# First norms of a fp32 encoder trunk: loads reordered, zero products on TensorE, operands written straight from PSUM, and sums of x placed later

## The chip, the cores and the metric

The kernel runs on one core of a Trainium2 chip. The metric is the device time of one execution in microseconds. A core has five engines that run their own instruction queues and wait for each other by semaphores: TensorE (PE in the profile, with its weight loads as PEld), VectorE (DVE), ScalarE (ACT), GpSimd (POOL) and SyncE (SP, which here only issues DMAs). ACT and POOL issue some DMAs too.

## The reference

Two sequences, 512 and 256 tokens of 1024 channels, go through the same two layers:

```python
def run_trunk(x, norm_g, final_norm_g, ffn_w1, ffn_w2, ...):
    for li in range(DEPTH):                      # DEPTH = 2
        x = x + 0.5 * swiglu_ffn(rmsnorm(x, norm_g[li, 0]), ffn_w1[li, 0], ffn_w2[li, 0])
        h = rmsnorm(x, norm_g[li, 1])
        x = x + (hgrn2_mixer(h, ...) if li == 0 else window_gqa_mixer(h, ...))
        x = x + 0.5 * swiglu_ffn(rmsnorm(x, norm_g[li, 2]), ffn_w1[li, 1], ffn_w2[li, 1])
    return rmsnorm(x, final_norm_g)

def rmsnorm(x, g):      # in float32
    return x * lax.rsqrt(jnp.mean(x * x, axis=-1, keepdims=True) + 1e-6) * g

def swiglu_ffn(x, w1, w2):
    gate, up = jnp.split(x @ w1, 2, axis=-1)     # w1: 1024 x 5632
    return (jax.nn.silu(gate) * up) @ w2         # w2: 2816 x 1024
```

So there are four feed-forward blocks (called f0 to f3 below), two token mixers and seven norms. The change touches the first norm, the start of f0, and one step of all four feed-forward blocks.

## The kernel before, in words

All 768 tokens are handled together as six blocks of 128 (`x[0]` to `x[5]`, 128 x 1024 each, in SBUF for the whole kernel); blocks 0 to 2 are half 0 and 3 to 5 half 1. A float32 product is made of three TensorE products: each operand is split into a high part (`hi`, rounded to the matmul's type) and a low part (`lo`, the difference), and `mm3` (L262 to L264) multiplies hi by hi, hi by lo, lo by hi. ACT makes the high part (L267, a cast), DVE the low part (L268, a subtraction); for weights the same is done at L170 and L171, and L203 and L204.

The kernel starts like this. `setup` loads an identity matrix (SP, L101) and casts it on DVE (L103); it loads the norm gains and some other vectors as rows into one tile (`cols`, three DMAs on ACT's queue, L109), turns them by a TensorE transpose (L112) and copies them out of PSUM on DVE (L114). `load_x` loads x (L278) and the first weights (L155). `norm_block` normalizes a block: ACT squares it and sums the row (L304), ACT takes the root (L305), DVE inverts it (L306) and scales x (L307) into `xn`. `turn` transposes four of the eight 128-channel columns of a half's three blocks (PE, L324), and multiplies by the gain while it copies out of PSUM (ACT, L327) into a plain tile `tn`. The six operands come from `tn`: first the parts of half 0 by `put`, which splits a pair of columns of 128 x 768 (L267, L268). In PE's order the plain products `up_plain` of half 0 come first, and between them, on fixed columns, `run_later` lets the deferred steps run: norms of half 1, its transposes, and `sums`.

The feed-forward products use a seven-product scheme on 2 x 2 blocks (`product`, L422), so that after the plain products sums of operands are needed: `mix` (L351 to L355, DVE on 128 x 768) and more splits; the tiles of this part are called t1 to t4. `up_pair` computes two hidden tiles with seven products, copies the first results out of PSUM on ACT (L439, L442), combines them on DVE (L448 to L461) and applies Silu (L445, L460); its tiles are split and, like the operands, mixed (L351 to L355 on 128 x 384 `tA` tiles). `down_quad` multiplies four hidden tiles back and adds to x (L508). Before its first use in a feed-forward block, six sums of quarters of x are made: three with L471 (`x12 += x22`) and three with L472 (`x21 -= x22`).

The program is written in one order, and a scheduler gives every engine its own queue from it, by when it reckons that an instruction can start; `issue_after(x)` puts instructions behind x in that order. Each engine then runs its queue strictly in order. Tiles come from rings by tag: `tB` has two buffers, so that the third tile of that tag waits until the first is free.

Of the kernel before, what the change touches and what calls it, by code (L numbers as in the profile page):

```python
# [9 lines left out]
F32 = mybir.dt.float32  # L10
F32R = mybir.dt.float32r
# [5 lines left out]
P = 128  # L17
# [25 lines left out]
RING = 1024  # L43
UP = ("p1", "p7", "p2", "p5", "p4", "p6", "p3")
# [4 lines left out]
class Trunk:  # L49
# [216 lines left out]
    def split(self, src, hi, lo):  # L266
        self.nc.scalar.copy(hi, src)  # L267
        self.nc.vector.tensor_sub(lo, src, hi.bitcast(F32))  # L268

    def load_x(self, srcs):  # L270
# [30 lines left out]
    def norm_block(self, b):  # L301
        nc = self.nc
        xn, r = self.big([P, D]), self.stat(1)
        nc.scalar.activation(xn, self.x[b], AF.Square, accum_out=r)  # L304
        last = nc.scalar.activation(r, r, AF.Sqrt, bias=self.eps, scale=1.0 / D).ins  # L305
        nc.vector.reciprocal(r, r)  # L306
        nc.vector.tensor_scalar(xn, self.x[b], r, None, ALU.mult)  # L307
        self.xn[b] = xn
        return last

    def turn(self, half, part, row):
# [8 lines left out]
        for m in range(4 * part, 4 * part + 4):  # L320
# [5 lines left out]
            if feeds_ffn:  # L326
                nc.scalar.activation(self.block(part, half, m % 4), pt, AF.Copy, scale=g)  # L327
                continue
            hi, lo = (self.h[m][:, i, half * H : (half + 1) * H] for i in range(2))
            nc.scalar.activation(hi, pt, AF.Copy, scale=g)  # L330
            nc.vector.scalar_tensor_tensor(lo, pt, g, hi.bitcast(F32), ALU.mult, ALU.subtract)  # L331
        if feeds_ffn:
            for kp in range(2):
                self.put(f"b{part}{half}", kp, self.tn[(part, half)][:, kp])
# [30 lines left out]
    xn = [None] * NBLK  # L365

# [32 lines left out]
    def up_plain(self, tag, j, half):  # L399
# [13 lines left out]
        self.nc.scalar.activation(t, pss[0], AF.Silu)  # L413
# [51 lines left out]
    def down_quad(self, tag, g, hid):  # L465
        nc = self.nc
        cols = lambda b, c: self.x[b][:, c * 512 : (c + 1) * 512]
        if g == 0:
            for i in range(HB):
                x12, x21, x22 = cols(HB + i, 0), cols(i, 1), cols(HB + i, 1)  # L470
                nc.vector.tensor_add(x12, x12, x22)  # L471
                nc.vector.tensor_sub(x21, x21, x22)  # L472
# [873 lines left out]
```

## Time and profile before

| what | value |
| --- | --- |
| time, median of 3 runs | 2764.35 us (2763.74 to 2765.22) |
| the profiled execution | 2764.33 us, of which its span is 2762.5 us and 1.83 us lie around it |
| granted TensorE clock | 0.999 of full speed over the span |
| PE busy | 2735.5 us (99%) |
| DVE, ACT, POOL busy | 2102.6 us (76%), 1326.6 us (48%), 309.4 us (11%) |
| first matmul of a product | 14.79 us after the span's start |
| first product of the seven-product scheme | 38.63 us |

The profile gives for each line of the kernel the instructions with their engine, output and inputs, how long they ran, and for how long the engine stood idle before them and for what. In the timeline a row is "start, duration, engine, line, operation", and a count `x4` merges four instructions that follow each other; the duration is then from the first one's start to the last one's end.

### The profile page before, as it was taken

To read this page: it belongs to the slowest core of one execution; us is meant where nothing else is said; L and a number is where in the kernel's file an instruction comes from. 1 tells how busy PE (TensorE), PEld (TensorE's weight loads), DVE (VectorE), ACT (ScalarE), POOL (GpSimd) and SP (SyncE) were. 2 spreads that over 40 slices of the span, in tenths; PEclk is the share of its full clock that TensorE was granted. 3 is DMA by queue.
4 is the path that set the end of the run, shared out by engine and by line. 5 is a ranking of instruction groups with operands and counts; after the bars stand their busy time and mean duration, and the time that the engine had idled before them with its cause. 6 is when DMAs were issued, how large, how long until landed. Compare 5 with 4: busy or idle time off the path is not lost.

```text
span 2762.5 us, 44483 instructions
## 1 busy us (share of the span) xinstructions
PE 2735.5 (99%) x17281; PEld 2481.5 (90%) x17281; DVE 2102.6 (76%) x3662; ACT 1326.6 (48%) x2479; POOL 309.4 (11%) x315
## 2 busy tenths in 40 slices
PE   8999999999999999999999999999999999999998
PEld 8999999888888889999999999999886789999997
DVE  7888788557477568777888878887846768788877
ACT  7444444456466354443446444444546654443444
POOL 1111211000000001121111112111000001221111
PEclk9999999999999999999999999999999999999999
DMA  5544554321110324465444355544512123555443
GB/s 160 135 117 116 138 134 119 118 67 40 55 47 25 122 62 114 112 143 133 118 120 109 83 131 138 133 115 115 146 53 77 47 62 81 134 137 128 120 112 107
DMA packets 330116, 291.63 MB, mean 106 GB/s; under 512 B 11608, under 2 KB 257840, under 8 KB 329904
## 3 DMA queue, kind: packets, MB, share of 16 engines
q1 hardware_dynamic: 294064, 212.43, 25.8%
q0 software_dynamic: 31680, 62.93, 13.4%
q10 hardware_dynamic: 4160, 13.42, 1.4%
q8 instruction: 135, 2.21, 0.3%
q14 instruction: 77, 0.63, 0.1%
HBM read 216.39 MB, written 9.44 MB: 82 GB/s over the span
## 4 chain that ended last, share of the span: by engine, by line
PE 85%; DVE 10%; ACT 3%; issue 2%; DMA 0%; DVEq 0%; ACTq 0%; SPq 0%
PE ps L422 32%; PE ps L486 21%; PE ps L262 9%; PE ps L263 9%; PE ps L264 9%; DVE w L204 2%; DVE big L268 2%; PE ps L682 1%; PE ps L1218 1%; PE ps L1157 1%; PE ps L827 1%; PE ps L1209 1%; ACT w L203 1%; DVE wr L217 1%; PE ps L324 1%
## 5 line engine op out<-in xcount | busy, mean ns | idle before, releaser
L422 PE MATMUL ps<-big,w 128*128 128x384 f32 x6720 | 1174.6, 335 | 3.4 <-ACT tA L439 2.7
L422 PEld LDWEIGHTS ps<-big,w 128*128 128x128 f32 x6720 | 1165.4, 188 | 10.9 <-ACT tA L439 9.1
L203 ACT CAST w<-wr 128x512 fp32r<-128x512 f32 x600 | 415.3, 707 | 699.8 <-DVE wr L217 376.3
L204 DVE TENSOR_TENSOR w<-wr,w 128x512 fp32r<-128x512 f32 (+1 forms) x520 | 452.8, 874 | 180.1 <-ACT w L203 153.9
L486 PE MATMUL ps<-w,big 128*128 128x512 f32 x2520 | 575.9, 389 | 1.2 <-DVE x L508 1.2
L486 PEld LDWEIGHTS ps<-w,big 128*128 128x128 f32 x2520 | 472.4, 188 | 99.6 <-ACT big L267 1.6
L508 DVE SCALAR_TENSOR_TENSOR x<-ps,x 128x512 f32<-128x512 f32 x468 | 303.5, 680 | 10.5 <-PE ps L264 10.0
L145 POOL DMA_DIRECT2D s<-wr x120 | 105.0, 875 | 1667.5 <-DMA wr<-in_ffn_w_dram 784.5
L262 PE MATMUL ps<-w,big 128*128 128x512 f32 x624 | 252.5, 405 | 0.3
L264 PE MATMUL ps<-w,big 128*128 128x512 f32 x624 | 244.6, 392 | 0.9 <-DVE big L331 0.9
L263 PE MATMUL ps<-w,big 128*128 128x512 f32 x624 | 244.4, 392 | 0.0
L262 PE MATMUL ps<-big,w 128*128 128x384 f32 (+2 forms) x640 | 219.2, 344 | 2.1 <-ACT big L267 1.3
L267 ACT CAST big<-tA 128x384 fp32r<-128x384 f32 x296 | 148.0, 513 | 149.3 <-DVE tA L454 69.0
L263 PE MATMUL ps<-big,w 128*128 128x384 f32 (+2 forms) x640 | 216.4, 338 | 0.9 <-DVE big L268 0.6
L264 PE MATMUL ps<-big,w 128*128 128x384 f32 (+2 forms) x640 | 215.6, 337 | 0.0
L268 DVE TENSOR_TENSOR big<-tA,big 128x384 fp32r<-128x384 f32 x296 | 183.0, 629 | 12.7 <-ACT big L267 11.6
L171 DVE TENSOR_TENSOR w<-wr,w 128x1024 fp32r<-128x1024 f32 x92 | 111.8, 1221 | 79.0 <-ACT w L170 73.1
L262 PEld LDWEIGHTS ps<-w,big 128*128 128x128 f32 x624 | 117.2, 188 | 29.3 <-issue 6.0
L170 ACT CAST w<-wr 128x1024 fp32r<-128x1024 f32 x92 | 96.5, 1052 | 97.8 <-PE ps L263 77.8
L204 POOL TENSOR_TENSOR w<-wr,w 128x512 fp32r<-128x512 f32 x80 | 123.3, 1541 | 177.5 <-ACT w L203 156.4
L264 PEld LDWEIGHTS ps<-w,big 128*128 128x128 f32 x624 | 117.1, 188 | 27.6 <-DVE big L331 1.7
L263 PEld LDWEIGHTS ps<-w,big 128*128 128x128 f32 x624 | 117.4, 188 | 21.8 <-issue 0.4
(163 smaller groups left out, 2899.6 us busy)
## 6 DMA issues: line engine op xcount, KB each, us to landing
wr<-in_ffn_w_dram SPq DMA_DIRECT2D x264, 512.0 KB, 3.9
s<-in_ffn_w_dram SPq DMA_DIRECT2D x120, 256.0 KB, 3.3
s<-wr POOLq DMA_DIRECT2D x120, 256.0 KB, 4.5
wr<-wr POOLq DMA_DIRECT2D x80, 256.0 KB, 3.7
wr<-in_hg_w_in_dram SPq DMA_DIRECT2D x40, 512.0 KB, 3.8
wr<-wr POOLq DMA_DIRECT2D x20, 512.0 KB, 4.6
spill<-x ACTq DMA_DIRECT2D x12, 512.0 KB, 2.7
x<-spill ACTq DMA_DIRECT2D x12, 512.0 KB, 3.3
```

The source lines that it names most:

```text
L145: self.nc.gpsimd.dma_start(out, src, accum_op=ALU.add)
L171: self.nc.vector.tensor_sub(lo, raw, hi.bitcast(F32))
L203: nc.scalar.copy(h, src)
L204: low = (eng or nc.vector).tensor_sub(l, src, h.bitcast(F32)).ins
L262: nc.tensor.matmul(out, a[0], b[0], start=first, stop=False)
L263: nc.tensor.matmul(out, a[0], b[1], start=False, stop=False)
L264: nc.tensor.matmul(out, a[1], b[0], start=False, stop=last)
L267: self.nc.scalar.copy(hi, src)
L268: self.nc.vector.tensor_sub(lo, src, hi.bitcast(F32))
L422: self.nc.tensor.matmul(ps, a[x], b[y], start=first and k == 0 and i == 0, stop=k == 3 and i == 2, skip_group_check=True,)
L486: nc.tensor.matmul(ps, a[x], w[y], start=name == chain and kp == 0 and q == 0, stop=kp == 1 and q == 2, skip_group_check=True,)
L508: self.nc.vector.scalar_tensor_tensor(x, ps, c, x, ALU.mult, ALU.add)
```

## The change

Six things are changed.

1. **Loads.** The identity is loaded by ACT's queue instead of SP's, so that SP begins with x. The small load for the attention sinks (`load_tables`) goes behind the second half's norms.
2. **Zeros.** DVE clears a 128 x 128 tile, and TensorE multiplies it by itself 15 times (L103 of the new kernel) into a PSUM bank that nobody reads. The tile is a third one of tag `tB`.
3. **A square on DVE.** Block 1's square and row sum is one DVE instruction instead of an ACT one.
4. **Straight operands.** Half 0's operands are no longer split from `tn`: ACT writes the high part and DVE the low part directly from the PSUM bank, times the gain (L345, L346), and `tn`, which `sums` still needs, is rebuilt as hi + lo by four additions on POOL (L352).
5. **Second norms.** The three norms of half 1 are ordered right behind the first half's work, and the first Silu behind them.
6. **Sums of x.** In all four feed-forward blocks the six sums before `down_quad` are put behind the last operand split (`self.mixed`).

The lines move: L101 to L114 become L105 to L120, L170/L171 become L176/L177, L203/L204 L209/L210, L262-264 L268-270, L267/L268 L273/L274, L304-L307 L313-L316, L324 L333, L327 L341, L351-355 L371-375, L413 L435, L422 L445, L439 L462, L448-L461 L471-L484, L471/L472 L495/L496, L508 L532.

```diff
@@ setup
+        zero = self.tmp(P)
+        nc.vector.memset(zero, 0.0)
         self.eps = cp.tile([P, 1], F32, name="eps")
         nc.vector.memset(self.eps, EPS)
+        idle = self.ps(P)
+        for _ in range(WARM):                                   # WARM = 15
+            nc.tensor.matmul(idle, zero, zero, start=True, stop=True)
+        raw = self.tmp(P)
+        nc.scalar.dma_start(raw, ident)
         warm = self.stat(1)
         nc.scalar.activation(warm, self.eps, AF.Sqrt)
-        raw = self.tmp(P)
-        nc.sync.dma_start(raw, ident)
@@ load_x
             with self.tc.issue_after(order) if order else nullcontext():
-                order = self.norm_block(b)
-        self.turn(0, 0, 0)
-        self.turn(0, 1, 0)
+                order = self.norm_block(b, b == 1)
+        self.turn(0, 0, 0, True)
         with self.tc.issue_after(order):
             self.stage_next()
             self.stage_next()
-        self.load_tables()
-
-        def rest():
-            for b in range(HB, NBLK):
-                self.norm_block(b)
-
-        self.later(rest, lambda: self.turn(1, 0, 0), lambda: self.turn(1, 1, 0), self.sums)
+        self.turn(0, 1, 0, True)
+        for b in range(HB, NBLK):
+            with self.tc.issue_after(order):
+                order = self.norm_block(b)
+        self.normed = order
+        with self.tc.issue_after(order):
+            self.load_tables()
+        self.later(lambda: self.turn(1, 0, 0), lambda: self.turn(1, 1, 0), self.sums)
@@ norm_block
-        nc.scalar.activation(xn, self.x[b], AF.Square, accum_out=r)
+        if on_dve:
+            nc.vector.tensor_tensor_reduce(xn, self.x[b], self.x[b], 1.0, 0.0, ALU.mult, ALU.add, r)
+        else:
+            nc.scalar.activation(xn, self.x[b], AF.Square, accum_out=r)
@@ turn
+            if straight:
+                key = (f"b{part}{half}", m % 4 // 2)
+                if key not in self.ops:
+                    self.ops[key] = self.big([P, 2, 2, H], F32R)
+                hi, lo = (self.ops[key][:, m % 2, i, :] for i in range(2))
+            elif feeds_ffn:
...
             nc.scalar.activation(hi, pt, AF.Copy, scale=g)
             nc.vector.scalar_tensor_tensor(lo, pt, g, hi.bitcast(F32), ALU.mult, ALU.subtract)
...
+            if straight:
+                self.block(part, half, 0)
+                hi, lo = (self.ops[(name, kp)][:, :, i, :].bitcast(F32) for i in range(2))
+                nc.gpsimd.tensor_add(self.tn[(part, half)][:, kp], hi, lo)
+            else:
+                self.put(name, kp, self.tn[(part, half)][:, kp])
@@ put
-        self.split(src, t[:, :, 0, :], t[:, :, 1, :])
+        self.mixed = self.split(src, t[:, :, 0, :], t[:, :, 1, :])
@@ up_plain
-        self.nc.scalar.activation(t, pss[0], AF.Silu)
+        with self.tc.issue_after(self.normed) if self.normed else nullcontext():
+            self.nc.scalar.activation(t, pss[0], AF.Silu)
+        self.normed = None
@@ down_quad
-                nc.vector.tensor_add(x12, x12, x22)
-                nc.vector.tensor_sub(x21, x21, x22)
+                with self.tc.issue_after(self.mixed):
+                    nc.vector.tensor_add(x12, x12, x22)
+                    nc.vector.tensor_sub(x21, x21, x22)
```

What the scheduler makes of it stands in the engines' queues. A row is line, operation, output and inputs, size, and in brackets the counters that it waits for; a number behind a name only tells tiles of one kind apart.

**The start, ACT.** ACT's queue from its first DMA to the first root, before:

```order
L120 DMA nsinks<-in_sw_sinks_dram 128x16
L99 ACT_TABLE_LOAD
L99 ACTIVATE stat_80<-eps 128x1 [waits DVE_49]
L109 DMA tB_86<-in_norm_g_dram 48x128
L109 DMA tB_86<-in_hg_lb_dram 32x128
L109 DMA tB_86<-in_hg_g_norm_dram 8x128
L304 ACTIVATE big_110,stat_111<-x_94 128x1024 [waits DMAHW2_49]
L305 ACTIVATE stat_111<-stat_111,eps 128x1 [waits Activation_49]
```

and now:

```order
L105 DMA tB_98<-in_ident_dram 128x128
L107 ACT_TABLE_LOAD
L107 ACTIVATE stat_100<-eps 128x1 [waits DVE_49]
L115 DMA tB_104<-in_norm_g_dram 48x128 [waits DMAHW1_49,DVE_49]
L115 DMA tB_104<-in_hg_lb_dram 32x128
L115 DMA tB_104<-in_hg_g_norm_dram 8x128
L313 ACTIVATE big_128,stat_129<-x_112 128x1024 [waits DMAHW0_49]
```

The three row loads now wait: for the identity's DMA and for DVE. `cols` is the third tile of tag `tB`, after the zeros and the raw identity.

**The start, DVE.** DVE's queue from the identity's cast to the second block's scaling, before:

```order
L103 CAST ident_r<-tB_82 128x128 [waits DMAHW1_49]
L306 RECIPROCAL stat_111<-stat_111 128x1 [waits Activation_49]
L307 TENSOR_SCALAR big_110<-x_94,stat_111 128x1024 [waits DMAHW2_49,DVE_49]
L114 COPY cols<-ps_90 128x88 [waits PE_49]
L306 RECIPROCAL stat_117<-stat_117 128x1 [waits Activation_49]
L307 TENSOR_SCALAR big_116<-x_96,stat_117 128x1024 [waits DMAHW4_49,DVE_49]
```

and now, as far as the subtraction of the second weight and past it:

```order
L109 CAST ident_r<-tB_98 128x128 [waits DMAHW1_49]
L311 ISA big_134,stat_135<-x_114 128x1024 [waits DMAHW2_49]
L120 COPY cols<-ps_108 128x88 [waits PE_49]
L315 RECIPROCAL stat_129<-stat_129 128x1 [waits Activation_49]
L316 TENSOR_SCALAR big_128<-x_112,stat_129 128x1024 [waits DMAHW0_49,DVE_49]
...
L177 TENSOR_TENSOR w_176<-wr_118,w_175 128x1024 [waits DMAHW7_49,Activation_49]
L346 SCALAR_TENSOR_TENSOR big_150<-ps_146,cols,big_150 128x384 [waits Activation_49]
...
L346 SCALAR_TENSOR_TENSOR big_163<-ps_166,cols,big_163 128x384 [waits Activation_49]
L177 TENSOR_TENSOR w_184<-wr_120,w_183 128x1024 [waits DMAHW0_49,Activation_49]
```

The copy of the gains (L114, now L120) stood behind the first block's scaling and now stands ahead of it.

**The sums of x, DVE.** The end of the stretch between operand sums and the first pair's combination, before:

```order
L448 TENSOR_TENSOR tA_593<-tA_593,ps_591 128x384 [waits PE_49]
L204 TENSOR_TENSOR w_656<-wr_400,w_656 128x512 [waits DMAHW4_49,Activation_49]
L217 TENSOR_TENSOR wr_398<-wr_398,wr_400 128x512 [waits DMASW3_49]
...
L452 TENSOR_TENSOR tA_592<-tA_592,ps_589 128x384 [waits PE_49]
...
L459 TENSOR_TENSOR tA_592<-tA_592,ps_591 128x384 [waits DVE_49,PE_49]
```

and now, with two more of the sums 16 and 20 rows above the first one shown:

```order
L471 TENSOR_TENSOR tA_615<-tA_615,ps_613 128x384 [waits PE_49]
...
L223 TENSOR_TENSOR wr_420<-wr_420,wr_422 128x512 [waits DMASW2_49]
L495 TENSOR_TENSOR x_124<-x_124 128x512
L496 TENSOR_TENSOR x_114<-x_114,x_124 128x512
L475 TENSOR_TENSOR tA_614<-tA_614,ps_611 128x384 [waits PE_49]
...
L482 TENSOR_TENSOR tA_614<-tA_614,ps_613 128x384 [waits DVE_49,PE_49]
...
L495 TENSOR_TENSOR x_126<-x_126 128x512
```

In f0, four of the six sums now stand between the operand sums and L482 (before: L459), in f1 to f3 all six. Before, all six stood ahead of the operand sums, among the norms.

More of the change, by code (lines that the diff above doesn't have):

```diff
@@ L43 @@
 RING = 1024
+WARM = 15
 UP = ("p1", "p7", "p2", "p5", "p4", "p6", "p3")
@@ L267, in split @@
         self.nc.scalar.copy(hi, src)
-        self.nc.vector.tensor_sub(lo, src, hi.bitcast(F32))
+        return self.nc.vector.tensor_sub(lo, src, hi.bitcast(F32)).ins
     def load_x(self, srcs):
@@ L309, in norm_block, with turn @@
         return last
-    def turn(self, half, part, row):
+    def turn(self, half, part, row, straight=False):
         nc = self.nc
@@ L365 @@
     xn = [None] * NBLK
+    normed = None
     def after_block(self, b, row):
```

11 lines of the change are left out of this document (5 added, 6 removed).

## The prediction

> **What bounds the kernel now.** I read the page first, then what PE waits for, then the timeline of the first 75 us.
>
> ```profile
> PE 2735.5 (99%) x17281; PEld 2481.5 (90%) x17281; DVE 2102.6 (76%) x3662; ACT 1326.6 (48%) x2479; POOL 309.4 (11%) x315
> PE ps L112 <- DMA tB<-in_hg_g_norm_dram: 7.2, 1, 7.2
> PE ps L422 <- ACT tA L439: 2.7, 11, 0.4
> ```
>
> PE is busy for 2735.5 of 2762.5 us; only 27 us can be won by waiting less. Most of what the waits show is at the start: 7.2 until the last row arrives. The one that comes back is L422 for ACT's copy L439, eleven times. So the change can move a few microseconds, in two places: the first 75 us, and the place in each feed-forward block where the second pair's first product waits for L439.
>
> The start, as the list of DMA issues (first row; 3.0 us from issue to landing) and the timeline have it:
>
> ```profile
> tB<-in_ident_dram SPq DMA_DIRECT2D x1, 64.0 KB, 3.0
> 1.25 0.38 ACTq L109 DMA_DIRECT2D tB<-in_norm_g_dram  x1
> 2.13 0.57 ACTq L109 DMA_DIRECT2D tB<-in_hg_g_norm_dram  x1
> 3.72 0.23 DVE L103 CAST ident_r<-tB 128x128 fp32r<-128x128 f32 x1 [2.85 <-DMA tB<-in_ident_dram]
> 7.23 0.38 PE L112 MATMUL ps<-ident_r,tB 88*128 88x88 f32 x1 [7.23 <-DMA tB<-in_hg_g_norm_dram]
> 7.95 0.24 DVE L114 COPY cols<-ps 128x88 f32<-128x88 f32 x1
> 8.09 5.38 PE L324 MATMUL ps<-ident_r,big 128*128 128x128 f32 x24 [0.48 <-DVE big L307]
> 10.02 0.75 DVE L307 TENSOR_SCALAR big<-x,stat 128x1024 f32<-128x1024 f32 x1
> 12.02 2.00 ACT L327 ACTIVATE big<-ps,cols 128x384 f32<-128x384 f32 x4 [0.90 <-PE ps L324]
> 15.78 0.45 PE L263 MATMUL ps<-big,w 128*128 128x384 f32 x1 [0.55 <-DVE big L268]
> 25.39 1.03 PE L324 MATMUL ps<-ident_r,big 128*128 128x128 f32 x8
> 27.72 0.75 DVE L307 TENSOR_SCALAR big<-x,stat 128x1024 f32<-128x1024 f32 x1
> 37.15 1.82 DVE L351 TENSOR_TENSOR big<-big,big 128x768 f32<-128x768 f32 x2
> ```
>
> The third norm ends at 10.77 (10.02 + 0.75), the first PSUM bank is read at 12.02, PE runs through from 15.78, the sixth norm ends at 28.47, and DVE begins the operand sums at 37.15. What comes then decides how much of an earlier start survives:
>
> ```profile
> 38.00:75.00 37.00, 36.56 (x211) 36.25 (x210) 35.73 (x53) 21.30 (x39) 5.88 (x4) 1.00 0.34 93
> 73.06 0.56 DVE L459 TENSOR_TENSOR tA<-tA,ps 128x384 f32<-128x384 f32 x1
> 74.08 0.46 ACT L439 COPY tA<-ps 128x384 f32<-128x384 f32 x1
> 74.59 0.65 PEld L422 LDWEIGHTS ps<-big,w 128*128 128x128 f32 x4 [0.75 <-ACT tA L439]
> ```
>
> In the first row (time share by stretch; columns PE, PEld, DVE, ACT, POOL) DVE is busy 35.73 of 37 us. At the end of that stretch DVE's L459 lets ACT's L460 and then L439 run, and PE has waited for them. So from 37.15 to 74.59 DVE, not PE, is the bound: a microsecond won for PE at 15.78 is worth nothing unless DVE reaches 37.15 earlier too and has no more to do behind it. The change does the first and spoils the second.
>
> **The change part by part. Loads, gains and the first norms.** x leads SP's queue now (the identity stood ahead of it), which brings block 0 some tenths earlier. But the row loads on ACT's queue wait for the identity's cast, since `cols` takes the raw identity's buffer. The cast ends at 3.95 (3.72 + 0.23); the third row load is issued 0.88 later (2.13 - 1.25), at 4.83. Before, it took 5.1 from issue to PE's start (7.23 - 2.13) with x in flight; the identity took 3.0. Bounds: 7.8 and 9.9; I take 8.9. From L112's start to the copy's end is 0.96 (7.95 + 0.24 - 7.23), so the gains are there at 9.85 (8.8 to 10.9). DVE now has this copy ahead of the first block's scaling, so x's earlier arrival and the square on DVE win nothing: all three blocks stand behind the copy, at about 0.95 each (0.75 and a reciprocal). The third norm ends at 12.7 (11.6 to 13.7), 1.9 later than before. Were the rows not late, the square on DVE would matter; its nearest row, a custom DVE instruction of 384 columns at 610 ns, gives 1.6 us for 1024 at most (0.8 if it went like the scaling's 0.75), either of which lies in the wait for the gains.
>
> ```profile
> L1173 DVE CUSTOM_DVE_ANT_0 big<-ps,big,nsinks 128x384 f32<-128x384 f32 x32 | 17.8, 610 | 1.2 <-PE ps L1157 1.0 <-PE ps L264 0.2
> L331 DVE SCALAR_TENSOR_TENSOR big<-ps,cols,big 128x384 fp32r<-128x384 f32 x32 | 17.9, 607 | 6.6 <-ACT big L330 6.4
> L330 ACT ACTIVATE big<-ps,cols 128x384 fp32r<-128x384 f32 x32 | 16.4, 583 | 11.4 <-PE ps L324 9.3 <-DMA spill<-x 2.2
> L170 ACT CAST w<-wr 128x1024 fp32r<-128x1024 f32 x92 | 96.5, 1052 | 97.8 <-PE ps L263 77.8
> L171 DVE TENSOR_TENSOR w<-wr,w 128x1024 fp32r<-128x1024 f32 x92 | 111.8, 1221 | 79.0 <-ACT w L170 73.1
> L304 ACT ACTIVATE big<-x 128x1024 f32<-128x1024 f32 x36 | 38.3, 1065 | 27.6 <-DVE x L506 12.7 <-DVE x L508 11.6 <-DMA x<-in_x_prompt_dram 2.9
> L304 ACT ACTIVATION_READ_ACCUMULATOR big<-x 128x1 f32 x36 | 6.9, 192 | 0.0
> 6.76 0.29 ACT L305 ACTIVATE stat<-stat,eps 128x1 f32<-128x1 f32 x1
> 17.05:20.50 3.45, 3.30 (x11) 2.80 (x10) 3.13 (x5) 3.45 (x5) 0.00 (x0) 0.51 1.17 290
> 13.60:17.05 3.45, 1.71 (x8) 1.46 (x9) 2.51 (x4) 3.45 (x7) 0.00 (x0) 1.00 1.09 340
> ```
>
> **Zeros and the clock.** The 24 transposes ran 0.22 us apart (5.38 / 24); eight at 25.39 took 1.03, 0.13 each. With zeros before them they might run at the faster pace. But the zeros end by 4.3 at that pace of 0.22 (15 x 0.22 from 1.0), by 7.6 if each takes two passes, and the first transposes come at 10.8. The last two rows above speak against them: a stretch in which PE was busy for 1.71 of 3.45 us was followed by one at a granted clock of 0.51. At the faster pace the first bank is read 0.4 behind the third norm, at 13.1; at the slower one the two blocks' 14 transposes pace it, 10.8 + 14 x 0.22 and half a microsecond, 14.3. I take 13.7.
>
> The Trainium skill, "TensorE: Matmul & The Clock Gate", section "Part 1: The HAM clock gate", says that the gate falls back to half rate after an idle window of about 3.4 us. By it the slower pace holds and the end below is 0.6 later than by the middle.
>
> **Straight operands.** From bank to operand it is now one ACT write and one DVE instruction, 0.58 + 0.61 and about 0.1 of signalling, 1.3 instead of 3.76 (15.78 - 12.02). PE runs through from 15.0, 0.8 earlier. What DVE still has before the sixth norm's end: 8 such instructions (4.9), three weight subtractions of 1.22 (3.7), three norms of 0.95 (2.9): 11.4 us from 14.3, 25.7. ACT has 8 writes (4.6), three casts of 1.05 (3.2), three squares with their sum's reading and root, 1.07 + 0.19 + 0.29 (4.7), 12.4 from 13.7: 26.1, and the last scaling behind it ends at 27.1. The first Silu and its table load now stand behind the last root; ACT has that gap while the second half is transposed, so two loads less are part of this 12.4 and win nothing more.
>
> **The additions on POOL.** Four of 128 x 768; the nearest is POOL's 128 x 512, of which the quickest of 80 takes 1282 ns (first row below), so 1.28 x 1.5 = 1.9 each undisturbed. They run from about 16 to 24, beside DVE's weight subtractions, and both read two SBUF inputs. What happens then stands in the timeline:
>
> ```profile
> L204 POOL TENSOR_TENSOR w<-wr,w x80: 1282/1612/2996, 48.4 to 2716.5; 128x512 fp32r<-128x512 f32 x80
> 48.40 1.91 POOL L204 TENSOR_TENSOR w<-wr,w 128x512 fp32r<-128x512 f32 x1 [10.95 <-ACT w L203]
> 49.07 1.78 DVE L204 TENSOR_TENSOR w<-wr,w 128x512 fp32r<-128x512 f32 x1
> 50.78 0.68 DVE L204 TENSOR_TENSOR w<-s,w 128x512 fp32r<-128x512 f32 x1
> ```
>
> DVE's 0.68 became 1.78: it ended half a microsecond after POOL's. So a collision costs 1.1, and between none and three (one for each subtraction) are possible: 0 to 3.3. I take one and a half, 1.5, since the reads from PSUM between them leave gaps: DVE 27.2, level with ACT's 27.1. The sixth norm then ends 1.3 earlier than 28.47, and with it the second half's transposes, its operands and the start of the operand sums: 37.15 becomes 35.9.
>
> **The sums of x.** Four now lie in f0's stretch, six in that of each other block. Their rows, and what idle time there is to take them up, in the same stretches of the four blocks:
>
> ```profile
> L471 DVE TENSOR_TENSOR x<-x 128x512 f32<-128x512 f32 x12 | 8.3, 689 | 0.2
> DVE w L204 <- ACT w L203: 1.0, 2, 0.8
> DVE w L204 <- ACT w L203: 2.5, 6, 0.8
> 1065.17 0.48 ACT L442 COPY tA<-ps 128x384 f32<-128x384 f32 x1 [0.42 <-PE ps L422]
> 1558.72 0.48 ACT L442 COPY tA<-ps 128x384 f32<-128x384 f32 x1 [1.50 <-PE ps L422]
> 2320.31 0.48 ACT L442 COPY tA<-ps 128x384 f32<-128x384 f32 x1 [0.57 <-PE ps L422]
> ```
>
> Back to back a sum takes 0.61 (of the row's 0.69 the first 0.08 overlap). f0: 4 x 0.61 = 2.4, less 1.0 idle: 1.4 later. f1: 6 x 0.61 = 3.7, less 2.5 idle (f1 and f3 alike, the second waits row), less the 0.42 by which ACT stood ahead of PE: 0.8 stays. f2 stood 1.50 ahead: nothing stays. f3 0.57: 0.6. Bounds for f1 to f3 together: 0 if the copy's lead and the idle grow with the norms being freed, and 8.5 (11.0 - 2.5) if no idle time lies behind the sums. I take 1.4, since most of that idle time is in the second half of the stretch. The saving where they stood is nothing: no wait of PE's names L471 or L472.
>
> **The sum**, against the profiled 2764.33 (of which the median is 0.02 off): start -1.3, f0's sums +1.4, f1 to f3 +1.4, together +1.5: **2765.8**. That is a start some tenths of a microsecond to one better for PE and nothing won at the end.
>
> **The rivals.** *The adds stay out of DVE's way* and the rows come early: 7.8 and the quick transposes bring ACT's 27.1 to 25.4, 3.1 earlier than before, and with f0's +1.4 and all other sums hidden the time is 2762.6; with f0's hidden too, 2761.2. For it: POOL's share is 11%, and reads from PSUM beside POOL aren't stretched. Against: three subtractions must all fall between four adds.
>
> *POOL holds DVE* (the other side): the adds run back to back as long as they are ready, and a subtraction that comes during the first waits for the next one too. Its place is DVE's L177 for the second and third weight; its price up to 1.9 per subtraction, 5.7 for three instead of 1.5. The start is then 2.9 later instead of 1.3 earlier, and the time 2770.0; with the gains at 10.9, 2771. It decides if L177 behind the fourth L346 ends more than 2 us after it starts. Against: in the rows above DVE came in as soon as one add ended.
>
> The Trainium skill, "SBUF — State Buffer", section "SBUF: two separate sides", has VectorE and GpSimd share a port pair as an exclusive lock for a whole instruction, taken by whoever comes first. The rows above agree for one add (1.78 against 0.68); none shows who is next when two are queued.
>
> *The sums of x are not taken up* in f1 to f3: up to 8.5, 2772.9. For it: DVE's queue is in order, and the copy L439 stands behind it on ACT. Against: the idle rows.
>
> *It doesn't do what it says*: the clock closes again behind the zeros, and the table loads were never on the path. That is half in my sum already and moves it by 0.6.
>
> **How the numbers follow.** A difference under 0.2% (5.5 us) isn't told from no change. My forecast (2763.5 to 2768): 0.55. Adds out of the way (2758.8 to 2763.5): 0.21; below 2758.8 everything at once would have to be better than my bounds, 0.07. POOL holds DVE: 0.1; sums not taken up: 0.07. Of these two half lie above 2769.9. The range reaches from 2760.5 to 2770.5. Faster 0.07, same 0.84, slower 0.09.
>
> **What would show it.** Right: PE's L118 later than 7.5 us; the gains' copy ahead of the first L316; the first L333 past 9.5; L177 at 1.8 us or more beside an L352 on POOL; operand sums (L371) at 35 to 37; a wait of L445 for L462 of over 0.5 us in f0, f1 and f3. Wrong: row loads landing before 7.5, DVE at L371 before 34, or no longer wait at L445 in the later blocks.

## The result: slower by 6.7 us, and the profile after

The changed kernel takes 2771.32 us (median of 10 runs, 2770.81 to 2772.64) against 2764.64 us of the kernel before (10 runs beside it): a ratio of 1.0025, 95% interval 1.0015 to 1.0035. The forecast was 2765.8 with a range up to 2770.5. The result lies above it, at what the rival "POOL holds DVE" priced (2770.0 to 2771).

The page's busy line and what PE waits for, in the changed kernel:

```profile
PE 2741.6 (99%) x17311; PEld 2484.8 (90%) x17311; DVE 2106.1 (76%) x3669; ACT 1319.1 (48%) x2471; POOL 334.6 (12%) x319
PE ps L118 <- DMA tB<-in_hg_g_norm_dram: 4.9, 1, 4.9
PE ps L445 <- ACT tA L462: 3.6, 10, 0.7
PE ps L333 <- DVE big L316: 3.2, 3, 1.3
PE ps L510 <- DVE x L532: 3.0, 4, 1.0
```

and the one wait of the kernel before of the last kind (L486 is now L510, L508 is L532):

```profile
PE ps L486 <- DVE x L508: 1.2, 1, 1.2
```

PE is busy 6.1 us longer, 5.3 of it with zeros. The down product's wait for the additions to x went from 1.2 to 3.0; the old wait of L422 for L439 (now L445 for L462) went from 2.7 to 3.6. The start, from the timeline:

```profile
1.05 5.34 PE L103 MATMUL ps<-tB 128*128 128x128 f32 x30 [1.05 <-DVE eps L100]
4.69 0.23 DVE L109 CAST ident_r<-tB 128x128 fp32r<-128x128 f32 x1 [3.68 <-DMA tB<-in_ident_dram]
5.81 0.57 ACTq L115 DMA_DIRECT2D tB<-in_hg_g_norm_dram  x1
11.33 0.27 PE L118 MATMUL ps<-ident_r,tB 88*128 88x88 f32 x1 [4.94 <-DMA tB<-in_hg_g_norm_dram]
11.64 0.25 DVE L120 COPY cols<-ps 128x88 f32<-128x88 f32 x1 [4.62 <-PE ps L118]
12.80 5.38 PE L333 MATMUL ps<-ident_r,big 128*128 128x128 f32 x24 [1.20 <-DVE big L316]
13.72 0.75 DVE L316 TENSOR_SCALAR big<-x,stat 128x1024 f32<-128x1024 f32 x1
16.30 2.00 ACT L345 ACTIVATE big<-ps,cols 128x384 fp32r<-128x384 f32 x4 [5.38 <-PE ps L333]
18.14 9.23 POOL L352 TENSOR_TENSOR big<-big 128x768 f32<-128x768 f32 x4 [17.70 <-DVE big L346]
18.31 0.37 PE L269 MATMUL ps<-big,w 128*128 128x384 f32 x1
19.27 1.81 DVE L177 TENSOR_TENSOR w<-wr,w 128x1024 fp32r<-128x1024 f32 x1 [0.16 <-ACT w L176]
23.14 2.54 DVE L177 TENSOR_TENSOR w<-wr,w 128x1024 fp32r<-128x1024 f32 x1
25.80 2.13 DVE L316 TENSOR_SCALAR big<-x,stat 128x1024 f32<-128x1024 f32 x1
30.03 0.76 DVE L316 TENSOR_SCALAR big<-x,stat 128x1024 f32<-128x1024 f32 x1
39.52 1.82 DVE L371 TENSOR_TENSOR big<-big,big 128x768 f32<-128x768 f32 x2
```

The last row of the gains arrives at 11.33 instead of 7.23, and everything hangs on it: third norm's end 14.47 (before 10.77), first bank read 16.30 (12.02), PE running through 18.31 (15.78). Straight operands give 1.7 of this back between bank and PE. Then POOL's four additions run back to back from 18.14 to 27.37, and three DVE instructions stretch beside them: 1.81, 2.54 and 2.13 instead of 1.22, 1.22 and 0.75. The sixth norm ends at 30.79 (28.47), and the operand sums start at 39.52 (37.15).

How late PE is at the same matmul in both traces (start after less start before), worked out from the two profiled executions:

```
time before, us    36     70     85     95    500   1050   1090   1245   1300   2000   2350   2754
shift, us        +1.95  +1.95  +2.19  +3.13  +3.95  +3.97  +5.85  +5.92  +4.25  +5.53  +6.11  +7.14
```

Two us are lost at the start, two in f0 behind it, and 3.2 net in f1 to f3. Between, in the first mixer (500 to 1050), nothing moves. The fall of 1.7 near 1255 is for the most part L486's wait of 1.2 us, which the kernel before had there and the new one hasn't; without that fall f1 to f3 lose 4.9.

The stretch of f0, the place of the second pair, and two of the new waits:

```profile
38.00:75.00 37.00, 37.00 (x215) 37.00 (x214) 36.98 (x56) 19.39 (x37) 6.56 (x4) 1.00 0.32 81
75.73 0.54 DVE L482 TENSOR_TENSOR tA<-tA,ps 128x384 f32<-128x384 f32 x1
76.27 0.47 ACT L462 COPY tA<-ps 128x384 f32<-128x384 f32 x1
76.79 5.47 PE L445 MATMUL ps<-big,w 128*128 128x384 f32 x30 [0.69 <-ACT tA L462]
91.41 0.68 DVE L532 SCALAR_TENSOR_TENSOR x<-ps,x 128x512 f32<-128x512 f32 x1
92.24 0.94 PE L510 MATMUL ps<-w,big 128*128 128x512 f32 x3 [0.65 <-DVE x L532]
1085.03 1.17 PE L510 MATMUL ps<-w,big 128*128 128x512 f32 x4 [0.98 <-DVE x L532]
```

DVE is busy for 36.98 of 37 us, 1.25 more than before: the four sums took all the idle time there was. PE waits 0.69 at the place instead of 0.43. But the larger loss is where the prediction didn't look: the down product waits for DVE's first addition to x (0.65 in f0, 0.98 in f1), since DVE comes late out of that stretch. Its two other waits lie late in f0 and f3 (0.51 at 442 us, 0.87 at 2691).

### The profile page after: what moved, and what is told of

Same layout as the page of the kernel before. It is cut to its first block, busy times and chain, and to the rows that moved or that the text cites. A ratio compares the mean times of both kernels' runs of the same rounds, so it can differ in the third digit from the quotient of the medians.

```text
span 2769.7 us, 44547 instructions
## 1 busy us (share of the span) xinstructions
PE 2741.6 (99%) x17311; PEld 2484.8 (90%) x17311; DVE 2106.1 (76%) x3669; ACT 1319.1 (48%) x2471; POOL 334.6 (12%) x319
## 4 chain that ended last, share of the span: by engine, by line
PE 85%; DVE 10%; ACT 2%; issue 2%; DMA 1%; DVEq 0%; ACTq 0%
PE ps L445 32%; PE ps L510 20%; PE ps L268 9%; PE ps L269 9%; PE ps L270 9%; DVE w L210 2%; DVE big L274 2%; PE ps L706 1%; PE ps L333 1%; PE ps L1242 1%; PE ps L1181 1%; PE ps L851 1%; PE ps L1233 1%; ACT w L209 1%; DVE wr L223 1%
## 5 line engine op out<-in xcount | busy, mean ns | idle before, releaser
L445 PE MATMUL ps<-big,w 128*128 128x384 f32 x6720 | 1175.4, 335 | 4.4 <-ACT tA L462 3.6
L445 PEld LDWEIGHTS ps<-big,w 128*128 128x128 f32 x6720 | 1165.2, 188 | 12.9 <-ACT tA L462 10.9
L209 ACT CAST w<-wr 128x512 fp32r<-128x512 f32 x600 | 414.6, 707 | 706.5 <-DVE wr L223 366.4
L210 DVE TENSOR_TENSOR w<-wr,w 128x512 fp32r<-128x512 f32 (+1 forms) x520 | 449.4, 868 | 177.6 <-ACT w L209 155.4
L510 PE MATMUL ps<-w,big 128*128 128x512 f32 x2520 | 577.3, 390 | 3.0 <-DVE x L532 3.0
L510 PEld LDWEIGHTS ps<-w,big 128*128 128x128 f32 x2520 | 472.0, 188 | 103.3 <-ACT big L273 4.8
L532 DVE SCALAR_TENSOR_TENSOR x<-ps,x 128x512 f32<-128x512 f32 x468 | 303.7, 682 | 10.3 <-PE ps L270 10.0
L268 PE MATMUL ps<-w,big 128*128 128x512 f32 x624 | 252.5, 405 | 0.3
L273 ACT CAST big<-tA 128x384 fp32r<-128x384 f32 x296 | 148.1, 513 | 152.6 <-DVE tA L477 70.2
L268 PE MATMUL ps<-big,w 128*128 128x384 f32 (+2 forms) x640 | 218.1, 343 | 0.0
L274 DVE TENSOR_TENSOR big<-tA,big 128x384 fp32r<-128x384 f32 x296 | 185.5, 637 | 12.4 <-ACT big L273 11.6
L177 DVE TENSOR_TENSOR w<-wr,w 128x1024 fp32r<-128x1024 f32 x92 | 113.9, 1243 | 80.1 <-ACT w L176 74.2
L210 POOL TENSOR_TENSOR w<-wr,w 128x512 fp32r<-128x512 f32 x80 | 138.6, 1732 | 184.5 <-ACT w L209 162.7
L268 PEld LDWEIGHTS ps<-w,big 128*128 128x128 f32 x624 | 117.2, 188 | 29.4 <-issue 5.6
L176 ACT CAST w<-wr 128x1024 fp32r<-128x1024 f32 x92 | 96.6, 1052 | 96.9 <-PE ps L269 77.7
L270 PEld LDWEIGHTS ps<-w,big 128*128 128x128 f32 x624 | 117.1, 188 | 27.6 <-DVE big L346 1.7
L151 POOL DMA_DIRECT2D wr<-wr x100 | 87.6, 876 | 447.9 <-ACT w L209 205.9
```

Source lines behind the costliest of these rows:

```text
L151: self.nc.gpsimd.dma_start(out, src, accum_op=ALU.add)
L177: self.nc.vector.tensor_sub(lo, raw, hi.bitcast(F32))
L209: nc.scalar.copy(h, src)
L210: low = (eng or nc.vector).tensor_sub(l, src, h.bitcast(F32)).ins
L268: nc.tensor.matmul(out, a[0], b[0], start=first, stop=False)
L270: nc.tensor.matmul(out, a[1], b[0], start=False, stop=last)
```

## The experiments

Each was timed against the kernel before on the same chip, with eleven runs of its own; an interval of such a ratio is about 0.09% (2.4 us) to either side. Differences of one to three microseconds between two of them aren't told apart by the times; there the traces are read, of which each shows one execution.

```
run                              rows    additions  sums of x     over the kernel before   95% interval of the ratio
the change                       late    POOL       new place     +6.7                     1.0015 to 1.0035
sums back                        late    POOL       old place     +5.1                     1.0010 to 1.0028
early rows                       early   POOL       new place     +0.1                     0.9992 to 1.0009
early rows, sums back            early   POOL       old place     +1.9                     0.9999 to 1.0017
no additions                     late    none       new place     +3.0                     1.0001 to 1.0018
additions on DVE                 early   DVE        new place     -2.2                     0.9982 to 1.0000
additions on DVE, sums back      early   DVE        old place     -3.2                     0.9980 to 0.9998
```

**Sums of x undone, and alone.** The first run is the changed kernel with

```diff
-                with self.tc.issue_after(self.mixed):
-                    nc.vector.tensor_add(x12, x12, x22)
-                    nc.vector.tensor_sub(x21, x21, x22)
+                nc.vector.tensor_add(x12, x12, x22)
+                nc.vector.tensor_sub(x21, x21, x22)
```

> The changed kernel with one part undone: the six sums of x are written without the order behind the last operand split, as in the kernel before. Theory S (the sums cost what was lost behind 70 us: in the changed trace the shift of PE against the kernel before grows from 1.95 at 70 us to 3.96 at 520 us and 7.14 at the end): 4 to 5.5 us less than the changed kernel's 2771.3, so 2766 to 2767.3, and the waits of the down product's first quad for L532 (0.65, 0.98, 0.87 us) are gone. Theory R (the later stalls come from the scheduler's new order and would be there without the sums): within 1 us of 2771.3. In both the shift at 70 us stays at 1.5 to 2.5.

and the second is the kernel before with the opposite edit:

> The kernel before with this one part of the change: the six sums of x behind the last operand split. Theory S: no shift at 70 us, then 4 to 5 us lost over the four feed-forward blocks, 2768.5 to 2769.5, with new waits of the down product for L508. Theory R: within 1 us of 2764.6.

Measured: 2770.37 beside 2765.31 (+5.1), and 2767.13 beside 2765.31 (+1.8, interval 0.9997 to 1.0015). The first is 0.95 under the change, within the microsecond that theory R gave; the second is neither theory's number. The shifts say why: with the sums back PE is 5.45 late at 70 us already and 5.51 at the end (1.9 lost on the way, and 1.8 won, almost all of it near 1255 as in the change). Against that run the change loses 1.4 in f0 and 3.7 behind it. So S was right on what happens behind 70 us, although some of the late waits aren't the sums' (L531, the same addition in that kernel, is still waited for at 445 and 2690 us, 0.52 and 0.47), and wrong on the start, where the sums cost 3.5 that they didn't cost before. With the sums alone PE is 0.37 late at 70 us and 4.43 at the end, in an execution 1.6 over that run's median. DVE in the timeline of the first of the two, and PE waiting there for the norm behind the sums:

```profile
18.35 8.71 POOL L352 TENSOR_TENSOR big<-big 128x768 f32<-128x768 f32 x4 [17.91 <-DVE big L346]
23.31 4.30 DVE L495 TENSOR_TENSOR x<-x,x 128x512 f32<-128x512 f32 x2
PE ps L333 <- DVE stat L315: 2.9, 1, 2.9
```

Two sums that take 0.69 each elsewhere took 4.30 together beside POOL's additions, ahead of the second half's norms. Where the change put them they were out of POOL's way and in DVE's fullest stretch instead.

**Early rows.** The zeros' tile is taken from another ring, so that the rows' tile doesn't wait for the raw identity's:

```diff
-        zero = self.tmp(P)
+        zero = self.tmp(H)[:, :P]
```

> The changed kernel with the tile of zeros taken from the eight tA buffers, so that the gains' rows have the second tB buffer and their loads wait for nothing. Theory W (the row loads' wait for the identity's cast sets the first norms): the gains' transpose starts at 7.5 to 8.5 instead of 11.33, the first product matmul at 14 to 15 instead of 17.84, and the time falls by 2.5 to 3.5 to 2768 to 2769. Rival (the rows are late because x's transfers fill the DMA engines, whenever they are issued): transpose still past 10, time within 1 us of 2771.3. If the zeros keep the clock up, the first 24 transposes are 0.13 apart and not 0.21.

Measured: 2765.43 beside 2765.31 (+0.1), 6.6 less than the change and more than either theory gave (in the traces it is 4.2 at 70 us and 4.4 at the end).

```profile
2.13 0.58 ACTq L115 DMA_DIRECT2D tB<-in_hg_g_norm_dram  x1
7.43 0.27 PE L118 MATMUL ps<-ident_r,tB 88*128 88x88 f32 x1 [0.50 <-DMA tB<-in_hg_g_norm_dram]
8.89 4.51 PE L333 MATMUL ps<-ident_r,big 128*128 128x128 f32 x24 [1.20 <-DVE big L316]
13.96 9.23 POOL L352 TENSOR_TENSOR big<-big 128x768 f32<-128x768 f32 x4 [13.51 <-DVE big L346]
18.95 2.54 DVE L177 TENSOR_TENSOR w<-wr,w 128x1024 fp32r<-128x1024 f32 x1
```

The rows are issued at 2.13 again and transposed at 7.43, 3.9 earlier. All that follows moves with it, POOL's hold included; PE's shift at 70 us is -2.25 instead of +1.95. So W is right and the rival wrong: from issue to use it was 5.3 here, 5.5 in the change and 5.1 before, so that here its start decided. (It is no fixed time: in the simplest version below, where no other load stands ahead of the rows on ACT's queue, the same row was used 3.2 us after its issue. Why isn't shown.)

**No additions.** POOL writes ones into the plain tiles instead of adding:

```diff
-                nc.gpsimd.tensor_add(self.tn[(part, half)][:, kp], hi, lo)
+                nc.gpsimd.memset(self.tn[(part, half)][:, kp], 1.0)
```

> The changed kernel in which POOL, instead of adding hi and lo into the plain operand tiles, writes ones into them (so the sums of operands in the first feed-forward block are not computed from the input; the instructions behind are the same). Theory P (a POOL instruction that reads two tiles holds DVE): DVE's weight subtractions take 1.2 instead of 1.81 and 2.54, the fourth block's scaling 0.75 instead of 2.13, the sixth norm ends about 3 us earlier, and the time falls by 1.5 to 3, to 2768.3 to 2769.8. Rival (ACT's squares and casts set the second half's norms): the sixth norm moves by less than 1 us and the time by less than 1.

Measured: 2768.28 beside 2765.31 (+3.0), 3.7 less than the change. DVE's instructions at the same places:

```profile
19.54 1.23 DVE L177 TENSOR_TENSOR w<-wr,w 128x1024 fp32r<-128x1024 f32 x1 [0.16 <-ACT w L176]
23.00 0.75 DVE L316 TENSOR_SCALAR big<-x,stat 128x1024 f32<-128x1024 f32 x1
24.77 1.23 DVE L177 TENSOR_TENSOR w<-wr,w 128x1024 fp32r<-128x1024 f32 x1 [1.03 <-ACT w L176]
28.28 0.76 DVE L316 TENSOR_SCALAR big<-x,stat 128x1024 f32<-128x1024 f32 x1
```

POOL's four writes wait for nothing and run at 0.74 to 3.50 us, so POOL computes nothing here. All of DVE's instructions are at their undisturbed time, and the sixth norm ends at 29.04, 1.75 earlier than in the change; PE's shift at 70 us is +0.20 instead of +1.95. In the third weight's wait for ACT (1.03) the rival shows: with POOL gone, ACT paces this stretch.

**No zeros, early rows with the sums back.** Without the zero products their tile is free at once, so this kernel has early rows too.

```diff
-WARM = 15
+WARM = 0
```

> The changed kernel without the zero products. Without them the zeros' tile is free at once, so that the rows' loads wait for nothing, as in the run with early rows (0.1 us over the kernel before there); between those two only the zeros differ. Theory B (the zeros cost the change their buffer and win next to nothing): the gains' transpose at 7 to 8 us, the 24 transposes 5.4 us long instead of 4.5, and the time 0 to 1 us over the run with early rows, about 0.5 over the kernel before. Rival (the warm clock is worth something): 2 us or more over the run with early rows. If the rows' wait were not the cause, the time would stay near 6.7 over the kernel before.

Measured: 2765.23 beside 2765.03 (+0.2): the same as early rows with zeros. The interval is 0.9991 to 1.0008. Theory B holds for this pair: its 24 transposes take 4.36 us without the zeros (not 5.4, as expected) and 4.51 with them, so that there the zeros sped nothing up; through their tile they cost the change what the rows' wait cost.

The next run joins the edit of the early rows and that of the sums back:

> The changed kernel with early rows and with the sums of x as in the kernel before; the additions stay on POOL. If the parts add up (early rows -6.6, sums back -1.6): 1.5 us under the kernel before. The shift of PE at 70 us should be about +1 (from -2.25 with early rows, and +3.5 for sums of x that stand beside POOL's additions, as in the run with the sums back), and nothing should be lost behind it. Rival (the sums hide in DVE's earlier gaps now): shift at 70 us of -2, 2 to 4 us under the kernel before.

Measured: 2766.89 beside 2765.03 (+1.9). The parts don't add up (-1.5 was expected). PE's shift at 70 us is +2.05, not +1, and little is lost behind it, in sum (+2.74 at the end). It is the same mechanism as with late rows: two sums take 4.31 us beside POOL's additions.

**Additions on DVE.** The four additions go to DVE, behind the second half's norms; with the sums back and without:

```diff
-                nc.gpsimd.tensor_add(self.tn[(part, half)][:, kp], hi, lo)
+                self.rebuild.append((self.tn[(part, half)][:, kp], hi, lo))
@@ load_x, behind the last norm
         with self.tc.issue_after(order):
             self.load_tables()
+            for out, hi, lo in self.rebuild:
+                nc.vector.tensor_add(out, hi, lo)
```

> As the run before in this list (early rows, sums of x as before), and the plain operand tiles rebuilt by four additions on DVE behind the second half's norms instead of on POOL. Theory P (POOL holds DVE): DVE's subtractions at 1.2 us, scalings at 0.75, shift of PE at 70 us -3 to -5, time 3 to 5 us under the kernel before. Rival (3.8 us more on DVE cost as much as POOL's hold did): no better than the run with additions on POOL.

> The changed kernel with early rows and the four additions on DVE, the sums of x behind the operand sums as the change has them. Against the run with early rows alone it differs by the additions' engine. Theory P: 2 to 4 us under it, so 2 to 4 under the kernel before; and 1.5 to 2 over the run with additions on DVE and sums of x as before (the price of the sums alone). Rival: the additions on DVE push the operand sums back and the time is that of the run with early rows or above.

Measured beside 2765.03: 2761.80 (-3.2, interval 0.9980 to 0.9998) and 2762.83 (-2.2). Theory P holds: against the same kernels with the additions on POOL, 5.1 and 2.3 less, although DVE has four instructions more. The 2.3 alone is inside the intervals, but PE's shift at 70 us is 5.2 and 2.7 less too. In the first one's timeline:

```profile
8.76 3.03 PE L336 MATMUL ps<-ident_r,big 128*128 128x128 f32 x24 [1.20 <-DVE big L319]
10.84 2.00 ACT L348 ACTIVATE big<-ps,cols 128x384 fp32r<-128x384 f32 x4 [0.65 <-PE ps L336]
13.81 1.23 DVE L177 TENSOR_TENSOR w<-wr,w 128x1024 fp32r<-128x1024 f32 x1
31.53 1.82 DVE L374 TENSOR_TENSOR big<-big,big 128x768 f32<-128x768 f32 x2
```

Operand sums start at 31.53 (37.15 before). PE's shift at 70 us is -3.1 with the sums back and -4.9 with the sums behind, and at the end -2.9 and -1.5: the new place of the sums wins 1.8 at the start and costs 3.4 later, against 0.2 with the old place. The difference of the two times, 1.0, is inside their intervals.

**Without the zeros again, and the identity's queue.** In the kernel above the transposes did run at the fast pace, so the zeros were taken away once more (`WARM` and their tile gone):

> Early rows, additions on DVE, sums of x as before (3.2 us under the kernel before), now without the zero products and their tile. In that kernel's trace the 24 transposes took 3.0 us, the fast pace, so here the zeros' clock could count. Theory C (the warm clock is worth what the transposes save): transposes 5.4 us long, first bank read 1 to 1.5 us later, time 1 to 2 us over it, 1 to 2 under the kernel before. Theory B (worth nothing, as between the two runs with additions on POOL): 3.2 under the kernel before, give or take 0.6.

Measured: 2762.85 beside 2765.23 (-2.4, interval 0.9983 to 1.0001). Its transposes take 4.47 us, not 5.4 as expected, and its first bank is read at 11.66, 0.8 later. The time is 0.8 worse, which the intervals don't tell from nothing; so neither theory is settled by it. In the trace PE is 2.5 later at 70 us without the zeros (-0.63 instead of -3.11), and 1.0 later at the end.

The identity's load back to SP in the changed kernel (`nc.sync.dma_start(raw, ident)`):

> The changed kernel with the identity's load back on SP's queue. The rows' loads still wait for its cast, but the scheduler now puts the gains' copy behind the scaling of the first two blocks on DVE. If the place of that copy ahead of the norms is what made late rows costly: the transposes of the first blocks start near 8, the first bank is read at 12 to 13.5 instead of 16.3, time 3 to 4.5 us less than the changed kernel, 2 to 4 over the kernel before. If the late rows cost the same wherever the copy stands (the multiplication by the gain needs them anyway): within 1.5 of the changed kernel.

Measured: 2770.05 beside 2765.23 (+4.8, interval 1.0009 to 1.0026), 1.9 less than the change: nearer to the second answer. PE's shift at 70 us is +1.19 instead of +1.95.

```profile
9.18 0.75 DVE L316 TENSOR_SCALAR big<-x,stat 128x1024 f32<-128x1024 f32 x1
11.94 0.38 PE L118 MATMUL ps<-ident_r,tB 88*128 88x88 f32 x1 [5.70 <-DMA tB<-in_hg_g_norm_dram]
12.11 5.33 PE L333 MATMUL ps<-ident_r,big 128*128 128x128 f32 x24
15.55 2.00 ACT L345 ACTIVATE big<-ps,cols 128x384 fp32r<-128x384 f32 x4 [3.38 <-PE ps L333]
```

The first norm is ready at 9.93, but PE's queue is in order, and the gains' transpose L118 stands ahead of the first L333: PE can't begin before 11.94. The order on DVE, on which I had put the blame, was only one of two queues in which the late rows stood in front.

**The simplest part alone.** Identity first on SP, no zeros, no square on DVE, sums at the old place; left are the straight operands, the additions on DVE, the second norms ahead of the Silu, and the small load for the sinks behind them. The second run below adds the zeros again, in a `tA` tile.

> Straight operands with the additions on DVE and the second norms ahead of the Silu, and nothing else of the change: the identity first on SP as before, no zeros, no square on DVE, sums of x as before. If the gain of 3.2 us comes from these two parts: 2 to 4 under the kernel before. If the loads' order and the square on DVE carry it: within 1 of the kernel before. Behind 70 us nothing should be lost.

> The best version so far (identity first on SP, no square on DVE, straight operands with additions on DVE, sums of x as before; 4.2 us under the kernel before), now with the 15 zero products, their tile among the tA buffers. Here the transposes start about 1.5 us behind the last zeros. If the warm clock counts where nothing else holds the transposes: the 24 transposes 3 us long instead of 4.4, the time 0.5 to 1.5 under that version, 4.7 to 5.7 under the kernel before. If not: 4.2 under it, give or take 0.6.

Measured: 2761.02 beside 2765.23 (-4.2, interval 0.9977 to 0.9995) and 2760.98 beside 2764.89 (-3.9, 0.9981 to 0.9999). Both beat both kernels. With the zeros the transposes take 2.95 us instead of 4.39 and PE is 0.8 earlier at 70 us (-3.24 instead of -2.46), but the time is the same.

```profile
4.90 0.38 PE L113 MATMUL ps<-ident_r,tB 88*128 88x88 f32 x1 [4.90 <-DMA tB<-in_hg_g_norm_dram]
7.85 4.39 PE L331 MATMUL ps<-ident_r,big 128*128 128x128 f32 x24 [2.58 <-DVE big L314]
```

In this version the rows' loads stand first on ACT's queue, since the sinks' load has left it, and are there at 4.90. That wins little: the transposes wait for the first norm (2.58) and start 0.24 earlier than before. So the identity on ACT's queue, the zeros and the square on DVE aren't needed for the gain. What the straight operands and the second norms' place are worth one by one, no run tells.

## Why the prediction was wrong, point by point

**What bounds the kernel.** Right: nothing won for PE counts unless DVE is earlier at the operand sums. In the change they start 2.37 later, and PE is 1.95 later at 70 us; in the best versions they start 5 to 6 earlier. Wrong was "the place in each feed-forward block": in f0 and f1 the down product's wait for L532 came beside L462's, with 0.65 and 0.98 us.

**Loads and gains: the step that failed.** Of the 5.6 us by which PE's shift at the end (7.14) missed the sum (1.5), 3.2 lie in the start, 0.6 in f0 and 1.8 in f1 to f3, and the start went wrong here first. The prediction named the wait (rows behind the identity's cast, the copy ahead of the norms) and mis-sized it. The cast: put at 3.95, its end was 4.92, since the identity, now on ACT's queue beside x, landed a microsecond later. From the last row's issue to its use: I took 4.0, between 3.0 (the identity's, issued ahead of x) and 5.1 (the same load's, beside x); it was 5.5. The row that is the same load under the same traffic was the one to take. Gains at 11.89 instead of 9.85, outside my bounds (8.8 to 10.9); the third norm at 14.47 instead of 12.7.

**Zeros and the clock.** The middle that I took (13.7 for the first bank) was no possible case: the pace was the slow one. PE had stood idle from 6.39 to 11.33, and the granted clock in the two stretches behind was 0.58 and 0.50:

```profile
11.00:14.50 3.50, 1.97 (x9) 1.84 (x10) 2.75 (x8) 0.00 (x0) 0.00 (x0) 0.58 1.02 389
14.50:18.00 3.50, 3.50 (x19) 3.50 (x18) 2.18 (x4) 1.70 (x4) 0.00 (x0) 0.50 1.17 295
```

The rule of the Trainium skill on an idle window, "TensorE: Matmul & The Clock Gate", section "Part 1: The HAM clock gate", held here. It isn't the whole of it: in the run with early rows PE had stood idle for 0.50 and 1.20 us only, and the granted clock from 9 to 13 us was 0.56 and 0.59 all the same, while with the additions on DVE, after idle times of 1.19 and 1.20, it was 1.00. What decides between the two isn't shown. Where the zeros did keep the pace up, the transposes went from 4.39 to 2.95 us, and the times show no gain.

**Straight operands.** From bank to PE's run 2.0 us (16.30 to 18.31) instead of 3.76; predicted 1.3. The mechanism is right: in the simplest version PE runs through from 13.09, 2.7 earlier than before and ahead of any second norm. With the additions elsewhere this and the second norms' place are the change's gain.

**The additions on POOL.** Predicted 1.9 each and 1.5 us of DVE's time in all. One by one they are:

```profile
18.14 1.86 POOL L352 TENSOR_TENSOR big<-big 128x768 f32<-128x768 f32 x1 [17.70 <-DVE big L346]
19.95 2.84 POOL L352 TENSOR_TENSOR big<-big 128x768 f32<-128x768 f32 x1
22.74 1.86 POOL L352 TENSOR_TENSOR big<-big 128x768 f32<-128x768 f32 x1
24.55 2.83 POOL L352 TENSOR_TENSOR big<-big 128x768 f32<-128x768 f32 x1
```

The first and third took the 1.9, the second and fourth a microsecond more, and DVE lost 0.59 + 1.32 + 1.38 = 3.3, my upper bound. The reason for 1.5 (one and a half collisions) fails: POOL always had an addition ready, and all three DVE instructions of that kind in this time were held. The third held was not a subtraction but a scaling, which reads one tile. Not all of the 3.3 reached PE, since ACT paces the stretch too: without the additions PE is 1.75 earlier at 70 us.

**The start in all:** -1.3 predicted, +1.95 at 70 us measured. The late rows account for 4.2 (the shift with early rows is -2.25), and that run differs from the change only in the zeros' tile, and so in when the rows may be loaded. The operand sums, put at 35.9, started at 39.52.

**Sums of x.** f0: +1.4 predicted; +1.2 from 70 to 95 us and another 0.8 by 500, but 1.4 against the run with the sums back, so this term fits. f1 to f3: +1.4 predicted, +3.2 in the profiled pair and 3.7 against the run with the sums back. That the times don't show so much (1.6 less without them in the change, 1.8 less with them and early rows; both inside the intervals) is because their old place cost 3.5 to 4.3 at the start as soon as POOL's additions stood there. Alone, on the kernel before, they cost 1.8, which is inside the interval too. The forecast priced the old place at nothing, by the trace of before, in which POOL did nothing there.

**The rivals.** "POOL holds DVE" gave 2770.0 to 2771, and the time is 2771.3, but not by its mechanism: no DVE instruction waited for two additions. Each got its turn when the addition that ran had ended (18.14 + 1.86 = 20.00; the subtraction that met it ended at 19.27 + 1.81 = 21.08), and the next addition was the longer for it. By its own sign it failed: L177 behind the fourth L346 took 1.81, not over 2. That the number fits is luck: its start would be +2.9 to +3.9, which was +1.95, and what it has for the sums of x (2.8) was 5.2. "Adds out of the way" was wrong in each part. In sum a chance of 0.09 for slower was too small, since late rows, slow clock and POOL's hold were treated as independent middles, while each stood at its worse end.

## What to carry to other kernels

A tile that is added to a short ring makes some later load wait, and a load that heads an in-order queue takes the whole start with it: look first at what each load now waits for. Price it by the same transfer under the same traffic, not by a middle. Work moved to GpSimd wasn't free here, since VectorE had work beside it that it held up; four instructions more on VectorE were 2 to 5 us cheaper.

## What the runs showed of the hardware

A VectorE scaling of one tile (`tensor_scalar`, 128 x 1024 float32) was held by a POOL addition as a subtraction of two tiles was: 2.13 us instead of 0.75, and 0.75 again in the run without additions, where POOL computed nothing at that time. The Trainium skill says that this can happen, in "SBUF — State Buffer", section "Who interferes with whom", which counts `tensor_scalar` among the operations that can take both ports; the prediction had counted only instructions with two inputs. Reads from PSUM with one SBUF operand (L346) weren't stretched: four took 2.18 beside the additions and 2.19 in the run without.

POOL and DVE took turns. The two subtractions ended 1.1 us after the addition that they had met (21.08 after 20.00, 25.68 after 24.60), nearly the 1.22 that they need alone, and the scaling 0.55 after its own; the additions that followed the subtractions took 2.84 and 2.83 instead of 1.86. Read from these durations, an addition that was ready waited in its turn for DVE's subtraction.

In five of the fourteen profiled executions (sums alone, early rows, no zeros, additions on DVE with the sums back, the simplest version with zeros) PE lost 1.2 to 1.6 us near 2085 us at a lower granted clock, as in the run with the sums alone:

```profile
2080.00:2100.00 20.00, 18.34 (x117) 12.95 (x117) 13.11 (x48) 13.56 (x42) 0.00 (x0) 0.91 0.27 84
```

So a shift at the end of one trace can differ from the medians by that much. The change, the run with the sums back and the kernel before have no such loss; what other differences of single executions are in the change's loss in f1 to f3 stays open.
